# Gates of eight tokens read from PSUM key by key; the second norm closed by VectorE in halves for every token block

## The chip, the cores and the metric

The kernel runs on one core of a Trainium2 chip. Its time is the time of one execution on the device in microseconds; lower is better. One execution before the change was profiled, and three more were timed without a profile.

## The reference, cut to what matters

One decoder layer over 512 tokens of width 1024: a token mixer (attention beside a linear recurrence), a layer norm, a PEER mixture of 16384 one-neuron experts, and a second layer norm. The parts that the change touches are the gates of the experts and the last norm:

```python
sc, ci = lax.top_k(cand, PEER_TOPK)
e1 = jnp.take_along_axis(i1, ci // PEER_TOPK, axis=-1)
e2 = jnp.take_along_axis(i2, ci % PEER_TOPK, axis=-1)
experts = (e1 * PEER_N_KEYS + e2).reshape(T, PEER_HEADS * PEER_TOPK)
gates = jax.nn.softmax(sc.astype(jnp.float32), axis=-1)...
act = jax.nn.gelu(jnp.einsum('cd,ced->ce', hc, u))
return jnp.einsum('ce,ced->cd', gc * act, peer_v[ec])
...
h = layer_norm(ALPHA * h + peer_ffn(h, ...), ln2_g, ln2_b)
```

Every token has 8 heads of 16 experts with a gate each. An expert's number is a pair of keys (e1, e2) of 128 each.

## The kernel before, in words

The 512 tokens are four blocks of 128. Three blocks (384 tokens) are computed densely: the gelu of all 16384 experts is made by TensorE, 128 experts at a time (a block of the table u; there are 128 of them), multiplied by a dense matrix of gates that is zero for experts not chosen, and multiplied by the table v, 128 experts at a time. The fourth block is done by gathering its chosen rows of u and v.

**The gate stage** lies in the trace between 355 and 600 us. It goes over the 384 tokens in 48 steps of 8 tokens. `onehots` (L897 to L919) makes for each token two one-hot matrices of its chosen keys, one of them scaled by the gates (VectorE L910, L917, L918, ScalarE L916). `gate_mm` multiplies them on TensorE (L927, L928), two matmuls for each token, into the PSUM tile `psg` of 8 tokens by 128 keys, with the keys of a token side by side; there are two such tiles, in turn. Then three instructions empty the tile:

- L936, ScalarE: keys 60 to 127 (68 of them) are copied to `gst`, a staging tile in SBUF with 16 tokens side by side for each key, which a DMA (L945) writes to memory every second step, for later.
- L939, VectorE: of keys 0 to 59, those `na` whose activations were made already are multiplied into these activations, in place, in the SBUF tile `act` (60 keys by 384 tokens, tokens side by side).
- L941, ScalarE: the rest of keys 0 to 59 are copied into `act`; when their activations come, they are multiplied by them (L275, L276).

All three go through a token's keys, and then to the next token. So they read PSUM in runs along the keys, and in SBUF each element is 16 tokens (`gst`) or 384 tokens (`act`) from the one before. `na` grows from 11 in the first step to 58 in the last: L939 has 88 to 464 elements in a partition, L941 392 to 16, and L936 always 544.

Between these, TensorE makes the activations of the next u blocks (`u_mm`, L206 to L208, `psu` and `psv`), each from a block that ScalarE and VectorE split into two halves of its precision (L202, L203).

**The v stage** (to about 1361 us): for each of 128 blocks of experts ScalarE and VectorE split the block of v (L1093, L1094) and the weights (L1099, L1101), and TensorE adds the products to six accumulators (L1056, L1058). The last seven blocks are held back, and multiplied block of tokens by block of tokens, so that the accumulators of the first tokens are complete earlier.

**The end**: `finish(t)` runs for t = 0 (the gathered tokens, `gacc`), 1, 2 and 3. It adds the residual (L1143 or L1148), makes mean and variance in `layer_stats` and the reciprocal root in `rsqrt` (small VectorE instructions, L215 to L234), and then, for t below 3, a small instruction for the shift (L1158), ScalarE's scale and shift of 1024 columns (L1159), VectorE's multiplication by the gain and addition of the bias (L1160, L1161; the two rows of parameters lie in `gr`) and one DMA (L1162). For t = 3 alone it is VectorE in two halves of 512 columns: subtract the mean and multiply by the gain (L1153), multiply by the root and add the bias (L1154), and one DMA for each half from the SP and the ScalarE queues (L1155).

Each engine runs its instructions in a fixed order, which a scheduler chose when the program was built.

Of the kernel before, what the change touches and what calls it, by code (L numbers as in the profile page):

```python
# [9 lines left out]
F32 = mybir.dt.float32  # L10
# [4 lines left out]
AF = mybir.ActivationFunctionType  # L15
OP = mybir.AluOpType
AX = mybir.AxisListType.X

P = 128
S = 512  # L20
D = 1024
NT = 4
# [22 lines left out]
NW = 60  # L45
# [99 lines left out]
def _program(ctx, tc, nc, a, out, dbg, stop):  # L145
    V, A, G, T = nc.vector, nc.scalar, nc.gpsimd, nc.tensor
# [19 lines left out]
    def mk(pool, shape, dt, tag, bufs):  # L166
        uid[0] += 1
        return pool.tile(shape, dt, name=f"{tag}_{uid[0]}", tag=tag, bufs=bufs)
# [58 lines left out]
    def layer_stats(pool, src, tag):  # L227
        st = mk(pool, [P, 2, 6], F32, tag + "st", 2)
        for i in range(2):
            V.bn_stats(st[:, i], src[:, i * 512:(i + 1) * 512])  # L230
        mv = mk(pool, [P, 2], F32, tag + "mv", 2)
        V.bn_aggr(mv, st)
        ve = mk(pool, [P, 1], F32, tag + "ve", 2)
        V.tensor_scalar(ve, mv[:, 1:2], EPS, None, op0=OP.add)  # L234
        return mv, rsqrt(pool, ve, tag)
# [3 lines left out]
    def raw4():  # L239
        return mk(rp, [P, 1024], F32, "raw", RAW_BUFS)  # L240
# [383 lines left out]
    for c in range(4):  # L624
        rnn_ssq(c, sqr[c])
    V.tensor_reduce(ssq.rearrange("p t k -> p (t k)"), ssp[:, :8 * NT].rearrange("p (a g) -> p a g", g=4), axis=AX,
                    op=OP.add)
# [11 lines left out]
    for c in range(DC):  # L639
        r = raw4()  # L640
# [69 lines left out]
    pp = ctx.enter_context(tc.tile_pool(name="pp", bufs=1))  # L710
# [165 lines left out]
    NB = 8  # L876
# [44 lines left out]
    GST = {}  # L921

    def gate_mm(col0, ob, oh, ol):
        o2 = mk(PB["g"][0], [P, NB, P], F32, "psg", PB["g"][1])
        for t in range(NB):
            q = (slice(None), t // R, slice(None), t % R)
            T.matmul(o2[:, t], ob[q], oh[q], start=True, stop=False)  # L927
            T.matmul(o2[:, t], ob[q], ol[q], start=False, stop=True)  # L928
        ch, q = divmod(col0, TCH)
        if q == 0:  # L930
            GST[0] = mk(gp, [P, NKEY - NW, TCH], F32, "gst", 2)

        def part(ap):
            return ap.rearrange("p e r -> p r e")

        A.activation(part(GST[0][:, :, q:q + NB]), o2[:, :, NW:], AF.Copy)  # L936
        na = min(nact[0], NW)
        wc = W[0][:, :, col0:col0 + NB]
        V.tensor_tensor(part(wc[:, :na]), part(wc[:, :na]), o2[:, :, :na], op=OP.mult)  # L939
        if na < NW:  # L940
            A.activation(part(wc[:, na:]), o2[:, :, na:NW], AF.Copy)  # L941
        ncol[0] = col0 + NB
        if q == TCH - NB:
            i = max(i for i in range(NQ) if cut[i] <= ch)
            nc.sync.dma_start(gscr[i][:, :, ch - cut[i]].rearrange("g p e t -> p g e t"),  # L945
                              GST[0].rearrange("p (g e) t -> p g e t", e=GE))
# [52 lines left out]
    for s in range(NS):  # L999
        i, k = divmod(s, SPT)  # L1000
        if k == 0:
            gen = first[order[1]] if i == 0 else experts(order[2]) if i == 1 else iter(())
        with tc.issue_after(last[0].ins):
            steps(gen, 99 if k == SPT - 4 else 2 if k < 4 else 1)
        if k == SPT - 1 and i + 1 < ND:
            gate_prep(order[i + 1])
        nxt = onehots(order[(s + 1) // SPT], (s + 1) % SPT * NB) if s + 1 < NS else None
        if nu[0] < NW - RES:
            u_block()
        gate_mm(s * NB, *pend)  # L1010
        pend = nxt
# [11 lines left out]
    def rows(*offs, scale=None):  # L1023
        rr = []
        for off in offs:
            r = mk(dg[0], [P, D], F32, "gr", GR_BUFS)
            nc.sync.dma_start(r, rowb(off, D))
            if scale is not None:
                A.activation(r, r, AF.Copy, scale=scale)
            rr.append(r)  # L1030
        return rr
# [37 lines left out]
    for b in range(NKEY):  # L1069
# [3 lines left out]
        g, k = divmod(b - NW, GE)  # L1073
# [21 lines left out]
        if b >= NW:  # L1095
            wc = w.rearrange("p (c t) -> p c t", t=TCH)
# [6 lines left out]
        if b == NKEY - NY:  # L1103
            l2g, l2b = rows(R_L2G, R_L2B)
            l1 = rows(R_L1G, R_L1B, scale=ALPHA)
            res = {}
            for t in range(NG, NT):
                y = raw4()
# [31 lines left out]
    def finish(t):  # L1140
        if t < NG:
            y = gacc[t]
            V.tensor_tensor(y, ah[t], gacc[t], op=OP.add)  # L1143
        else:
            y = res[t]
            for hf in range(2):
                sl = slice(hf * 512, hf * 512 + 512)
                V.scalar_tensor_tensor(y[:, sl], acc[t - NG][hf], 1.0 / GS, y[:, sl], op0=OP.mult, op1=OP.add)  # L1148
        mv, ri = layer_stats(pp, y, "ln2")
        if t == NT - 1:  # L1150
            for hf in range(2):
                sl = slice(hf * 512, hf * 512 + 512)
                V.scalar_tensor_tensor(y[:, sl], y[:, sl], mv[:, 0:1], l2g[:, sl], op0=OP.subtract, op1=OP.mult)  # L1153
                V.scalar_tensor_tensor(y[:, sl], y[:, sl], ri, l2b[:, sl], op0=OP.mult, op1=OP.add)  # L1154
                (nc.sync, nc.scalar)[hf].dma_start(out[t * P:(t + 1) * P, sl], y[:, sl])  # L1155
            return
        nm = mk(pp, [P, 1], F32, "ln2nm", 2)
        V.scalar_tensor_tensor(nm, mv[:, 0:1], -1.0, ri, op0=OP.mult, op1=OP.mult)  # L1158
        A.activation(y, y, AF.Identity, scale=ri, bias=nm)  # L1159
        V.tensor_tensor(y, y, l2g, op=OP.mult)  # L1160
        V.tensor_tensor(y, y, l2b, op=OP.add)  # L1161
        nc.sync.dma_start(out[t * P:(t + 1) * P], y)  # L1162

    for t in range(NT - 1):
        finish(t)
    with tc.high_priority():
        finish(NT - 1)
# [15 lines left out]
```

## Time and profile before

| | |
|---|---|
| median of 3 runs | 1375.07 us (1374.76 to 1376.82) |
| the profiled execution | 1375.56 us |
| its span, first to last instruction | 1373.8 us |
| busy over the span: TensorE matmuls | 1327.5 us, 97% |
| VectorE | 1192.3 us, 87% |
| ScalarE | 678.6 us, 49% |
| the chain that ended last | PE 76%, DVE 18%, ACT 2%, issue 2%, DMA 2% |
| mean granted TensorE clock | 0.989 |

The span is 1.76 us shorter than the profiled execution, which is 0.49 us above the median. In the profile PE is TensorE, DVE VectorE, ACT ScalarE, and a row such as `act<-act,psg 128x384` is an instruction that reads the tiles act and psg and writes act, with 384 elements in each of 128 partitions. Matmuls overlap, so their mean durations are longer than the time from one to the next.

### The profile page before, as it was taken

How to read it: one execution, taken by the hardware profiler on the slowest of the kernel's cores; microseconds unless marked ns; L12 is line 12 of the kernel's file. 1: busy time of each engine (PE TensorE's matmuls, PEld its weight loads, DVE VectorE, ACT ScalarE, POOL GpSimd, SP SyncE). 2: the span in 40 equal slices, each digit the busy share in tenths (PEclk: the TensorE clock that was granted, in tenths of full speed). 3: DMA queues.
4: the chain of work that ended last, by engine and by line, in shares of the span. 5: the costliest groups of instructions: out<-in, count | busy, mean ns of one | idle time of the engine just before them, and what ended most of it. 6: DMA issues, size and time to landing. Idle time of an engine off the chain costs nothing.

```text
span 1373.8 us, 21409 instructions
## 1 busy us (share of the span) xinstructions
PE 1327.5 (97%) x7601; PEld 721.3 (53%) x7601; DVE 1192.3 (87%) x2555; ACT 678.6 (49%) x1155; POOL 394.8 (29%) x300
## 2 busy tenths in 40 slices
PE   8999999998999989999999999999999999999996
PEld 3554555554666656655555555555555554444442
DVE  7956766899899998989898888888898889988887
ACT  5755165434798877765433333333333333333341
POOL 0103412300000000000654545445454555545400
PEclk9998999999999999999999999999999999999998
DMA  8103053223465564665999999999999999998851
GB/s 308 64 16 123 3 176 118 93 74 123 129 167 158 145 173 135 167 228 183 394 408 396 356 355 369 364 365 366 367 361 358 351 346 365 354 330 306 305 207 74
DMA packets 142859, 332.49 MB, mean 242 GB/s; under 512 B 62880, under 2 KB 63392, under 8 KB 142752
## 3 DMA queue, kind: packets, MB, share of 16 engines
q1 hardware_dynamic: 105168, 195.59, 42.4%
q0 software_dynamic: 36864, 134.23, 26.4%
q8 instruction: 59, 0.97, 0.3%
q10 hardware_dynamic: 720, 1.31, 0.3%
q14 instruction: 48, 0.39, 0.1%
HBM read 313.53 MB, written 17.56 MB: 241 GB/s over the span
## 4 chain that ended last, share of the span: by engine, by line
PE 76%; DVE 18%; ACT 2%; issue 2%; DMA 2%; POOL 0%; DVEq 0%; SPq 0%; ACTq 0%; POOLq 0%
PE psv L1056 22%; PE psv L1058 11%; PE psu L208 8%; PE psu L206 8%; PE psu L207 8%; PE psv L206 3%; PE psv L207 3%; PE psv L208 3%; DVE wl L203 3%; DVE oab L910 2%; PE psv L475 2%; DVE k L917 1%; PE psv L661 1%; PE psv L662 1%; PE psv L663 1%
## 5 line engine op out<-in xcount | busy, mean ns | idle before, releaser
L715 POOL DMA_INDIRECT gr<-u,ei x128 | 162.7, 1271 | 524.8 <-ACT act L278 369.6
L206 PE MATMUL psu<-hh,wh 128*128 128x384 f16 (+2 forms) x816 | 265.4, 326 | 7.1 <-ACT wh L202 3.0
L208 PE MATMUL psu<-hh,wl 128*128 128x384 f16 (+1 forms) x816 | 265.7, 326 | 5.1 <-DVE wl L203 5.1
L207 PE MATMUL psu<-hl,wh 128*128 128x384 f16 (+1 forms) x816 | 265.6, 326 | 0.0
L202 ACT ACTIVATE wh<-raw 128x1024 f16<-128x1024 f32 (+1 forms) x141 | 147.8, 1048 | 193.7 <-PE psu L207 150.1
L1056 PEld LDWEIGHTS <-w_h 128*128 128x128 f16 x1536 | 150.3, 98 | 173.5
L203 DVE SCALAR_TENSOR_TENSOR wl<-raw,wh 128x1024 f16<-128x1024 f32 (+1 forms) x141 | 171.3, 1215 | 66.1 <-ACT wh L202 65.8
L715 POOL DMA_INDIRECT gr<-v,ei x128 | 170.6, 1333 | 164.7 <-DVE gacc L967 144.4
L1099 ACT ACTIVATE w_h<-act 128x384 f16<-128x384 f32 x128 | 66.1, 521 | 255.7 <-PE psv L1056 254.3
L206 PEld LDWEIGHTS <-wh 128*128 128x128 f16 x1232 | 121.4, 99 | 102.6 <-ACT wh L202 9.4
L1056 PE MATMUL psv<-vl,w_h 128*128 128x512 f16 x582 | 173.4, 379 | 0.0
L1058 PE MATMUL psv<-vh,w_l 128*128 128x512 f16 x582 | 173.4, 379 | 0.0
L208 PEld LDWEIGHTS <-wl 128*128 128x128 f16 x1232 | 121.2, 98 | 99.0 <-DVE wl L203 9.1
L1056 PE MATMUL psv<-vh,w_h 128*128 128x512 f16 x582 | 171.6, 379 | 0.0
L207 PEld LDWEIGHTS <-wh 128*128 128x128 f16 x1232 | 121.4, 99 | 94.3 <-issue 7.9
L967 DVE SCALAR_TENSOR_TENSOR gacc<-gr,gact,gacc 128x1024 f32<-128x1024 f32 x127 | 162.4, 1279 | 0.7
L957 DVE SCALAR_TENSOR_TENSOR gr<-gr,ah 128x1024 f32<-128x1024 f32 x128 | 154.0, 1216 | 1.4 <-DMA gr<-u,ei 1.3
L1094 DVE TENSOR_TENSOR vl<-rv,vh 128x1024 f16<-128x1024 f32 x97 | 118.1, 1218 | 7.6 <-ACT vh L1093 7.6
L1058 PEld LDWEIGHTS <-w_l 128*128 128x128 f16 x768 | 75.1, 98 | 90.6
L208 PE MATMUL psv<-hh,wl 128*128 128x384 f16 (+2 forms) x352 | 119.8, 342 | 1.9 <-DVE wl L203 1.9
L206 PE MATMUL psv<-hh,wh 128*128 128x384 f16 (+2 forms) x352 | 119.8, 342 | 1.5 <-ACT act L278 0.8
L207 PE MATMUL psv<-hl,wh 128*128 128x384 f16 (+2 forms) x352 | 119.9, 342 | 0.0
(264 smaller groups left out, 2050.3 us busy)
## 6 DMA issues: line engine op xcount, KB each, us to landing
raw<-uT SPq DMA_DIRECT2D x128, 512.0 KB, 4.8
rv<-v SPq DMA_DIRECT2D x98, 512.0 KB, 6.8
raw<-v SPq DMA_DIRECT2D x30, 512.0 KB, 7.1
gs<-gst SPq DMA_DIRECT2D x24, 544.0 KB, 4.2
gsb<-gs SPq DMA_DIRECT2D x34, 384.0 KB, 8.5
raw<-w_q SPq DMA_DIRECT2D x16, 512.0 KB, 4.2
raw<-w_in SPq DMA_DIRECT2D x13, 512.0 KB, 4.8
raw<-w_out SPq DMA_DIRECT2D x8, 512.0 KB, 4.3
```

The costliest lines, as they stand in the source:

```text
L202: A.activation(hi, raw, AF.Copy, scale=WS)
L203: V.scalar_tensor_tensor(lo, raw, WS, hi, op0=OP.mult, op1=OP.subtract)
L206: T.matmul(o, lh, rh, start=first, stop=False)
L207: T.matmul(o, lh, rl, start=False, stop=False)
L208: T.matmul(o, ll, rh, start=False, stop=last)
L715: G.indirect_dma_start(out=r, out_offset=None, in_=table, in_offset=bass.IndirectOffsetOnAxis(ap=idx, axis=0))
L957: V.scalar_tensor_tensor(r, r, 1.0 / ALPHA, ah[t], op0=OP.mult, op1=OP.mult, accum_out=gact[t][:, j:j + 1])
L967: V.scalar_tensor_tensor(gacc[t], r, gact[t][:, j:j + 1], gacc[t], op0=OP.mult, op1=OP.add)
L1056: T.matmul(acc[t][hf], w_h[:, tt], vv[:, hf * 512:hf * 512 + 512], start=f and vv is vh, stop=False)
L1058: T.matmul(acc[t][hf], w_l[:, tt], vh[:, hf * 512:hf * 512 + 512], start=False, stop=l)
L1094: vs = V.tensor_tensor(vl, rv, vh, op=OP.subtract)
L1099: A.activation(w_h, w, AF.Copy)
```

## The change

The three instructions that empty the gate tile go through the keys, and for each key through its eight tokens; the shapes turn from 8 x keys to keys x 8. The number of instructions, their engines and the elements that they move stay. In SBUF an instruction now meets eight neighbouring tokens (32 bytes), then the next key; in PSUM each element is 128 elements (512 bytes) from the one before. And `finish` closes every block of tokens as it closed the last one alone.

```diff
-        def part(ap):
-            return ap.rearrange("p e r -> p r e")
-
-        A.activation(part(GST[0][:, :, q:q + NB]), o2[:, :, NW:], AF.Copy)
+
+        ok = o2.rearrange("p t k -> p k t")
+        A.activation(GST[0][:, :, q:q + NB], ok[:, NW:], AF.Copy)
         na = min(nact[0], NW)
         wc = W[0][:, :, col0:col0 + NB]
-        V.tensor_tensor(part(wc[:, :na]), part(wc[:, :na]), o2[:, :, :na], op=OP.mult)
+        V.tensor_tensor(wc[:, :na], wc[:, :na], ok[:, :na], op=OP.mult)
         if na < NW:
-            A.activation(part(wc[:, na:]), o2[:, :, na:NW], AF.Copy)
+            A.activation(wc[:, na:], ok[:, na:NW], AF.Copy)
...
         mv, ri = layer_stats(pp, y, "ln2")
-        if t == NT - 1:
-            for hf in range(2):
-                sl = slice(hf * 512, hf * 512 + 512)
-                V.scalar_tensor_tensor(y[:, sl], y[:, sl], mv[:, 0:1], l2g[:, sl], op0=OP.subtract, op1=OP.mult)
-                V.scalar_tensor_tensor(y[:, sl], y[:, sl], ri, l2b[:, sl], op0=OP.mult, op1=OP.add)
-                (nc.sync, nc.scalar)[hf].dma_start(out[t * P:(t + 1) * P, sl], y[:, sl])
-            return
-        nm = mk(pp, [P, 1], F32, "ln2nm", 2)
-        V.scalar_tensor_tensor(nm, mv[:, 0:1], -1.0, ri, op0=OP.mult, op1=OP.mult)
-        A.activation(y, y, AF.Identity, scale=ri, bias=nm)
-        V.tensor_tensor(y, y, l2g, op=OP.mult)
-        V.tensor_tensor(y, y, l2b, op=OP.add)
-        nc.sync.dma_start(out[t * P:(t + 1) * P], y)
+        for hf in range(2):
+            sl = slice(hf * 512, hf * 512 + 512)
+            V.scalar_tensor_tensor(y[:, sl], y[:, sl], mv[:, 0:1], l2g[:, sl], op0=OP.subtract, op1=OP.mult)
+            V.scalar_tensor_tensor(y[:, sl], y[:, sl], ri, l2b[:, sl], op0=OP.mult, op1=OP.add)
+            (nc.sync, nc.scalar)[hf].dma_start(out[t * P:(t + 1) * P, sl], y[:, sl])
```

Lines behind the first edit move up by one (L936 becomes L935, L939 L938, L941 L940, L1094 L1093, L1148 L1147; L1153 and L1154 become L1151 and L1152).

In the gate stage no instruction changes its place on any engine; TensorE's order is the same in the whole program. A piece of VectorE's order there (`psg` is the gate tile, `oab`, `k` and `gl`, `gh` belong to the one-hot matrices, `act` are the activations):

```order
 L276 TENSOR_TENSOR act_1888<-act_1888,utmp_3664 128x16
 L910 TENSOR_TENSOR oab_3766<-iota_1895,eT_3376 128x2048
-L939 TENSOR_TENSOR act_1888<-act_1888,psg_3668 128x8x13
+L938 TENSOR_TENSOR act_1888<-act_1888,psg_3668 128x13x8
 L918 TENSOR_TENSOR k_633_3703<-oab_3700,gl_579_3384 128x512
 L917 TENSOR_TENSOR k_632_3702<-oab_3700,gh_3380 128x1024
```

Only the shape is another: 13 keys of 8 tokens instead of 8 tokens of 13 keys.

At the end VectorE's order does change. Before, from the variance of the gathered tokens (`ln2ve_13755`) to the residual of the next block (`raw_13569`; `gr_13605` and `gr_13615` are the low halves of the last two blocks of v, `gr_13559` and `gr_13561` gain and bias):

```order
L234 TENSOR_SCALAR ln2ve_13755<-ln2mv_13753 128x1
L1094 TENSOR_TENSOR gr_13605<-rv_13603,gr_13605 128x1024
...
L1094 TENSOR_TENSOR gr_13615<-raw_13613,gr_13615 128x1024
...
L1158 SCALAR_TENSOR_TENSOR ln2nm_13769<-ln2mv_13753,ln2y_13757 128x1
L1160 TENSOR_TENSOR gacc_1210_7467<-gacc_1210_7467,gr_13559 128x1024
L1161 TENSOR_TENSOR gacc_1210_7467<-gacc_1210_7467,gr_13561 128x1024
L1148 SCALAR_TENSOR_TENSOR raw_13569<-psv_6913,raw_13569 128x512
```

The same stretch now:

```order
L234 TENSOR_SCALAR ln2ve_13755<-ln2mv_13753 128x1
L1151 SCALAR_TENSOR_TENSOR gacc_1210_7467<-gacc_1210_7467,ln2mv_13753,gr_13559 128x512 x2
L1093 TENSOR_TENSOR gr_13605<-rv_13603,gr_13605 128x1024
...
L1093 TENSOR_TENSOR gr_13615<-raw_13613,gr_13615 128x1024
L216 TENSOR_SCALAR ln2y_13757<-ln2w_13758 128x1
...
L1152 SCALAR_TENSOR_TENSOR gacc_1210_7467<-gacc_1210_7467,ln2y_13757,gr_13561 128x512 x2
L1147 SCALAR_TENSOR_TENSOR raw_13569<-psv_6913,raw_13569 128x512
```

The two halves of L1151 stand ahead of the low half of v's block 126, and of the small instructions of the root only two (L215, L217) now stand ahead of that of block 127 instead of five. ScalarE's last three instructions before (L1159 for t = 0, 1 and 2) are gone, and four DMAs of half a block stand there in place of one.

## Rows read from the trace of the kernel before

**Rows 1.** Stretches: us; busy (instructions) of PE, PEld, DVE, ACT, POOL; PEclk, DMA, GB/s.

```profile
355.00:435.00 80.00, 79.17 (x674) 54.16 (x673) 76.14 (x206) 74.71 (x160) 0.00 (x0) 1.00 0.58 155
435.00:495.00 60.00, 56.70 (x449) 37.30 (x448) 59.97 (x155) 50.91 (x108) 0.00 (x0) 1.00 0.61 163
495.00:540.00 45.00, 40.51 (x321) 26.36 (x320) 40.55 (x72) 31.67 (x71) 0.00 (x0) 0.96 0.53 144
540.00:600.00 60.00, 56.94 (x462) 37.76 (x460) 53.34 (x71) 43.90 (x104) 0.00 (x0) 0.97 0.61 162
600.00:1310.00 710.00, 710.00 (x3692) 361.05 (x3690) 631.07 (x890) 281.22 (x384) 333.31 (x256) 1.00 0.94 349
```

**Rows 2.** PE groups, 355 to 600 us: busy us, mean ns | idle before, releasers.

```profile
L206 PE MATMUL psu<-hh,wh 128*128 128x384 f16 x204 | 67.6, 332 | 1.6 <-ACT act L278 1.6
...
L206 PE MATMUL psv<-hh,wh 128*128 128x384 f16 x171 | 55.7, 326 | 1.5 <-ACT act L278 0.8 <-DVE gT L886 0.7
L927 PE MATMUL psg<-k,oab 128*128 128x128 f16 x384 | 47.6, 218 | 8.0 <-DVE k L917 4.4 <-ACT gst L936 2.1 <-ACT act L941 1.1
```

**Rows 3.** Groups of L939 and L936 in the same stretch.

```profile
L939 DVE TENSOR_TENSOR act<-act,psg 128x88 f32<-128x88 f32 (+47 forms) x48 | 35.1, 735 | 2.2 <-ACT gst L936 2.2
...
L936 ACT ACTIVATE gst<-psg 128x544 f32<-128x544 f32 x48 | 50.5, 1127 | 1.6 <-PE psg L928 1.5
```

**Rows 4.** Single forms of DVE and ACT, for rates (L1097 from 600 us on).

```profile
L939 DVE TENSOR_TENSOR act<-act,psg 128x384 f32<-128x384 f32 x1 | 1.0, 987 | 0.0
...
L276 DVE TENSOR_TENSOR act<-act,utmp 128x384 f32<-128x384 f32 x1 | 0.6, 550 | 0.0
...
L276 DVE TENSOR_TENSOR act<-act,utmp 128x88 f32<-128x88 f32 x1 | 0.2, 249 | 0.0
...
L1097 DVE TENSOR_TENSOR act<-act,gsb 128x384 f32<-128x384 f32 x68 | 37.4, 550 | 0.0
...
L941 ACT ACTIVATE act<-psg 128x384 f32<-128x384 f32 x1 | 0.8, 841 | 0.0
...
L275 ACT ACTIVATE utmp<-psu 128x384 f32<-128x384 f32 x2 | 0.9, 472 | 0.0
```

**Rows 5.** L939 by stretch: 435 to 495, 495 to 540, 540 to 600 us.

```profile
L939 DVE TENSOR_TENSOR act<-act,psg 128x216 f32<-128x216 f32 (+11 forms) x12 | 8.3, 695 | 0.0
...
L939 DVE TENSOR_TENSOR act<-act,psg 128x312 f32<-128x312 f32 (+7 forms) x8 | 7.0, 881 | 0.0
...
L939 DVE TENSOR_TENSOR act<-act,psg 128x368 f32<-128x368 f32 (+12 forms) x13 | 13.8, 1072 | 1.0 <-ACT gst L936 1.0
```

**Rows 6.** Timeline of the end: start us, us, engine, instruction [idle before, releaser].

```profile
1342.76 1.22 DVE L1094 TENSOR_TENSOR gr<-raw,gr 128x1024 f16<-128x1024 f32 x1 [0.89 <-ACT gr L1093]
1342.81 1.03 PE L1056 MATMUL psv<-gr,w_h 128*128 128x512 f16 x4
...
1346.25 1.23 DVE L1160 TENSOR_TENSOR gacc<-gacc,gr 128x1024 f32<-128x1024 f32 x1 [1.31 <-ACT gacc L1159]
...
1348.66 1.28 DVE L1148 SCALAR_TENSOR_TENSOR raw<-psv,raw 128x512 f32<-128x512 f32 x2
...
1351.16 0.21 DVE L232 BATCH_NORM_AGGREGATE ln2mv<-ln2st 128x2 f32<-128x12 f32 x1
...
1360.51 0.38 PE L1058 MATMUL psv<-gr,w_l 128*128 128x512 f16 x1
...
1362.81 1.23 DVE L1160 TENSOR_TENSOR raw<-raw,gr 128x1024 f32<-128x1024 f32 x1 [0.70 <-ACT raw L1159]
...
1365.68 0.20 DVE L232 BATCH_NORM_AGGREGATE ln2mv<-ln2st 128x2 f32<-128x12 f32 x1
...
1365.99 1.40 DVE L1153 SCALAR_TENSOR_TENSOR raw<-raw,ln2mv,gr 128x512 f32<-128x512 f32 x2
1367.31 0.14 DVE L215 TENSOR_SCALAR ln2w<-ln2ve 128x1 int32<-128x1 int32 x1
...
1369.02 1.41 DVE L1154 SCALAR_TENSOR_TENSOR raw<-raw,ln2y,gr 128x512 f32<-128x512 f32 x2
```

## The prediction

> **What bounds the kernel now.** First the stretches of the span [rows 1]. From 600 to 1310 us TensorE is busy 710.00 of 710 us, so a microsecond won before 600 us moves all of this forward, and nothing that ScalarE or VectorE save inside it counts; the change touches nothing there. In the gate stage, 355 to 600 us, TensorE stands 0.8, 3.3, 4.5 and 3.1 us in the four stretches (length less busy time), 11.7 us in all, and the granted clock falls to 0.96 and 0.97 in the last two: 45 x 0.04 + 60 x 0.03 = 3.6 us of full-speed time. VectorE is busy 76.14 of 80 and 59.97 of 60 us in the first two, 40.55 of 45 and 53.34 of 60 us in the others; ScalarE has 201.2 of 245. So VectorE paces the middle of the stage and TensorE the rest of it, nearly level. Next, what TensorE waited for there [rows 2]: 8.0 us ahead of the gate matmuls (4.4 for VectorE's one-hot product L917, 2.1 for L936 and 1.1 for L941, which hold the gate tile) and the other 3.7 us ahead of u's matmuls, mostly for ScalarE's L278. L939 and L936 are thus part of what it waits for: 35.1 us of VectorE and 50.5 us of ScalarE [rows 3]. Last the end [rows 6]: TensorE's last matmul starts at 1360.51 us, but VectorE still normalises the blocks before, and reaches the last block's variance (L232) only at 1365.68. The end hangs on VectorE.
>
> **The gate tile: what an element costs.** With 384 elements L939 takes 987 ns, and the same multiplication of neighbouring elements, L276, 550 [rows 4]. L276 goes from 249 ns at 88 elements to 550 at 384, 1.02 ns an element over about 160 ns, so an element of L939 costs (987 - 160)/384 = 2.15 ns. ScalarE shows the same: L941 841 ns, L275 472, with equal elements. In both slow rows PSUM is read side by side and SBUF is touched far apart, so SBUF is what doubles the price. Short runs in SBUF are not dear: L1097 reads gsb in runs of 16 tokens at 550 ns, as fast as L276 [rows 4]. Runs of eight floats should do as well.
>
> What no row shows is a read of PSUM with 512 bytes between elements. Its cost lies between about 1.0 ns, the price of a PSUM read side by side (L1148 of the end, 1.28 us for two times 512 [rows 6], with 0.1 us taken off for each), and 2.15 ns, what SBUF takes for far elements; nothing excludes more. I take 1.02. The reason is an estimate: from 600 to 1310 us 3692 matmuls of 384 or 512 columns fill 710 us [rows 1], 0.192 us each, so PSUM takes at least 384/192 = 2.0 columns in a nanosecond. An engine that draws one element in 1.02 ns asks for half of that, and could do so even if a far element spoiled its neighbour's place.
>
> [...]
>
> **What it saves.** L939 at 160 + 1.02 ns an element, by stretch [rows 5]: 12 instructions of 260 elements on average go from 695 to 425 ns, 3.2 us; 8 of 340 from 881 to 507, 3.0 us; 13 of 416 from 1072 to 584, 6.3 us. TensorE stood 3.3, 4.5 and 3.1 us there, so the smaller of the two in each is 3.2 + 3.0 + 3.1 = 9.3 us. I take four fifths, 7.5 us: in the last two stretches VectorE itself stood idle 4.5 and 6.7 us, so some waits are chains between engines that a faster L939 shortens only in part. The first stretch, with 0.8 us of idle TensorE, I leave out, and the clock too. ScalarE's saving is larger, about 0.5 us for each of 48 L936 (1127 x 472/841 = 630 ns), 24 us, but ScalarE has 44 us to spare; it counts through the gate tile, which comes free sooner. Bounds of this term: nothing, and 11.7 + 3.6 = 15 us. The staging DMA starts earlier and moves the same bytes; no order changes in this stage.
>
> **The end, followed row by row** [rows 6]. From one start to the next, a pair of halves costs 1.32 us (L1153 at 1365.99, L215 at 1367.31) and the root from L215 to the pair behind it 1.71 (to 1369.02). L1151 for the gathered tokens now stands ahead of the low halves of v's last two blocks. Its 1.32 us, less three small instructions that move behind, fit into the 0.89 us for which VectorE waited for ScalarE before the second low half, so that one starts at 1342.76 as before, and the first is done by then. TensorE comes to these two blocks at 1342.81 and uses the low half third, at about 1343.2: it isn't delayed. From 1342.76: 1.14 for the low half (its 1.22 less the 0.08 by which neighbours overlap, as in the 1.40 of L1153's pair), 1.54 for what is left of the root (without L215 and L217), 1.32 for L1152. So the next block's residual (L1148, now L1147) begins at 1346.76 instead of 1348.66; the 1.31 us wait for ScalarE ahead of L1160 is gone. A block then costs 2.50 for residual and statistics (1348.66 to L232 at 1351.16), 0.31 from L232 to L1151 (as 1365.68 to 1365.99), 1.32, 1.71 and 1.32 again: 7.16 us, and the block after it begins at 1353.92. That one takes the same and, among its small instructions, the first half of the last block's residual and statistics, 1.25 more: 1362.33. TensorE's last matmul starts at 1360.51 and takes 0.38, so it isn't waited for. The last half of residual and statistics, 1.25, and L232 starts at 1363.58 instead of 1365.68. What follows is the same. **2.1 us** off. Bounds: nothing, if six smaller DMAs on two queues in place of three delay the last two, and 3.5 us, where TensorE's end (1360.89 + 1.25) would bind. ScalarE's queue then holds DMAs alone, so their waits delay nobody.
>
> **Sum.** 1375.56 (the profiled execution) - 7.5 - 2.1 = 1365.96 us. This execution lay 0.49 us above the median of the runs, so I forecast **1365.5 us**.
>
> **Rivals.**
> - PSUM read far apart costs what SBUF did, 2.15 ns. For it: nothing in the trace shows the contrary, and two memories beside one engine may be built alike. Against it: the matmul estimate. The gate stage stays, the end gives 2.1: 1375.07 - 2.1 = 1373.0 us.
> - The reads are cheap, but TensorE's waits stay for the most part, since u's chain (L275 waits for L276, L278 lets u's matmuls go) and ScalarE are late next. For it: 3.7 of 11.7 us of waits are not ahead of gate matmuls [rows 2]. Against it: L276 stands behind L939 on VectorE. A third of the 7.5, and the 2.1: 1370.5 us.
> - Slower: a far PSUM element costs more than a far SBUF element, say another 1.02 ns. L939 meets 12 x 260 + 8 x 340 + 13 x 416 = 11248 elements where VectorE paces, which is 11.5 us more, and less the 2.1 of the end 1375.07 + 9.4 = 1384.5 us. It decides from 2.1 us / 11248 = 0.19 ns above the present 2.15 on. For it: each key's eight tokens lie 512 bytes apart over the whole tile, a pattern no row has. Against it: the slow SBUF rows stop at twice the price.
>
> **Chances and range.** Cheap reads and the waits go: 0.45. Cheap reads, waits mostly stay: 0.12. Price as now: 0.30. Dearer: 0.13. What a measurement can tell from no change is about 0.2%, 2.75 us. The first two are faster (0.57), the third, 2.1 us, is within it (0.30), the last is slower (0.13). The range goes from 1361.5 (11.5 us in the gate stage and the 2.1) to 1375.5, which holds the third case with a lost end; left out are the dearer case and a gain near the bound of 15. The forecast's own range is 1361.5 to 1369.
>
> **What would show it.** Right: L936's successor near 0.63 us and L939's at 384 elements near 0.55; TensorE idle under 5 us between 355 and 600 us, and the v stage about 7 us earlier; L232 of the last block about 2.1 us nearer to TensorE's end than its 5.2 us (1360.51 to 1365.68), with no wait for ScalarE among the blocks. Wrong: these durations at 1.1 and 0.99 us or above, or shorter ones with TensorE idle as before.

## The result, and the profile after

| | before | after |
|---|---|---|
| median | 1375.94 us (4 runs, 1374.76 to 1377.52) | 1361.2 us (4 runs, 1359.69 to 1361.63) |
| the profiled execution | 1375.56 us | 1361.63 us |
| its span | 1373.8 us | 1359.9 us |
| TensorE / VectorE / ScalarE busy | 1327.5 / 1192.3 / 678.6 us | 1323.4 / 1179.7 / 653.4 us |

The ratio to before is 0.9885, with a 95% interval of 0.9873 to 0.9897: 14.2 to 17.5 us faster. I had forecast 1365.5 us, 9.6 less, in a range that began at 1361.5. The direction and the mechanism held; what TensorE wins in the gate stage was sized too small.

TensorE runs the same 7601 matmuls in the same order in both kernels, so the start of one and the same matmul in the two traces tells where the time went:

| matmul that starts before at | after at | difference | won since the row above |
|---|---|---|---|
| 355.12 us | 356.74 us | +1.61 | |
| 435.16 | 435.97 | +0.81 | 0.8 |
| 495.08 | 491.77 | -3.30 | 4.1 |
| 540.05 | 533.37 | -6.68 | 3.4 |
| 600.03 | 588.49 | -11.54 | 4.9 |
| 1310.00 | 1298.46 | -11.54 | 0.0 |
| last, 1360.51 | 1348.97 | -11.54 | 0.0 |
| end of the span, 1373.8 | 1359.9 | -13.9 | 2.4 |

The gate stage gave 13.2 us, the end 2.4; the 1.6 us lost ahead of 355 us are a difference between two executions: in the other runs below this number goes from 0.4 to 3.5 us, where nothing was changed either. In this execution of the changed kernel the granted clock was 0.83 from 190 to 200 us and from 340 to 350 us, where it was 1.00 before. From 600 us on the difference stays the same until TensorE is done.

The price of the elements, in the lines of the changed kernel that answer to [rows 3, 4] (the groups of the gate stage, and single forms):

```profile
L938 DVE TENSOR_TENSOR act<-act,psg 128x88 f32<-128x88 f32 (+47 forms) x48 | 20.6, 431 | 0.1
...
L935 ACT ACTIVATE gst<-psg 128x544 f32<-128x544 f32 x48 | 29.5, 628 | 6.4 <-PE psg L928 6.0
L940 ACT ACTIVATE act<-psg 128x392 f32<-128x392 f32 (+47 forms) x48 | 15.2, 324 | 1.8 <-DVE act L938 1.8
...
L938 DVE TENSOR_TENSOR act<-act,psg 128x384 f32<-128x384 f32 x1 | 0.5, 547 | 0.0
...
L940 ACT ACTIVATE act<-psg 128x384 f32<-128x384 f32 x1 | 0.5, 471 | 0.0
```

VectorE's 384 elements take 547 ns instead of 987, about as many as L276 takes for neighbours in SBUF (550); ScalarE's take 471 instead of 841, as L275 does (472); and L935 takes 628 instead of 1127. The 512 bytes between elements in PSUM add nothing that these rows show: ScalarE's L275 reads PSUM side by side, and takes 472 ns where L940 takes 471. VectorE gives up 35.1 - 20.6 = 14.5 us, ScalarE's L936 50.5 - 29.5 = 21 us.

What TensorE waited for from 355 to 600 us (the PE groups with idle time before them), and the four stretches of [rows 1]:

```profile
L206 PE MATMUL psu<-hh,wh 128*128 128x384 f16 x224 | 73.0, 326 | 0.5 <-ACT act L278 0.5
L208 PE MATMUL psu<-hh,wl 128*128 128x384 f16 x223 | 72.7, 326 | 0.8 <-DVE wl L203 0.8
...
L206 PE MATMUL psv<-hh,wh 128*128 128x384 f16 x175 | 57.0, 326 | 0.9 <-DVE gT L886 0.7 <-ACT act L278 0.2
L927 PE MATMUL psg<-k,oab 128*128 128x128 f16 x384 | 47.0, 218 | 1.0 <-DVE k L917 1.0
```

```profile
355.00:435.00 80.00, 79.83 (x679) 54.63 (x678) 76.44 (x210) 67.12 (x161) 0.00 (x0) 1.00 0.58 162
435.00:495.00 60.00, 60.00 (x495) 40.52 (x494) 59.93 (x161) 46.85 (x114) 0.00 (x0) 1.00 0.62 169
495.00:540.00 45.00, 42.40 (x342) 28.00 (x341) 39.91 (x73) 31.16 (x81) 0.00 (x0) 1.00 0.56 156
540.00:600.00 60.00, 59.62 (x469) 39.19 (x468) 51.90 (x88) 43.21 (x105) 0.00 (x0) 1.00 0.68 205
```

Ahead of the gate matmuls 1.0 us is left of 8.0 [rows 2], and neither gate-tile copy of ScalarE is named any more. The granted clock is 1.00 in the last two stretches, where it was 0.96 and 0.97. In the second stretch VectorE is as busy as before (59.93 us, 59.97 then), but TensorE no longer waits for it: it is busy 60.00 of 60 us.

The end, from the changed kernel's timeline:

```profile
1333.71 1.42 DVE L1152 SCALAR_TENSOR_TENSOR gacc<-gacc,ln2y,gr 128x512 f32<-128x512 f32 x2
1335.04 1.28 DVE L1147 SCALAR_TENSOR_TENSOR raw<-psv,raw 128x512 f32<-128x512 f32 x2
...
1348.97 0.38 PE L1057 MATMUL psv<-gr,w_l 128*128 128x512 f16 x1
...
1350.49 0.68 DVE L1147 SCALAR_TENSOR_TENSOR raw<-psv,raw 128x512 f32<-128x512 f32 x1
1351.20 0.69 DVE L230 BATCH_NORM_STATS2 ln2st<-raw 128x6 f32<-128x512 f32 x1
1351.93 0.21 DVE L232 BATCH_NORM_AGGREGATE ln2mv<-ln2st 128x2 f32<-128x12 f32 x1
```

The last block's variance comes 2.96 us behind TensorE's last matmul, where it came 5.17 behind [rows 6]; I had counted 3.07.

### The profile page after: what moved, and what is told of

It reads as the page before. It is cut to its first block, busy times and chain, and to the rows that moved or that the text cites. A ratio compares the mean times of both kernels' runs of the same rounds, so it can differ in the third digit from the quotient of the medians.

```text
span 1359.9 us, 21413 instructions
## 1 busy us (share of the span) xinstructions
PE 1323.4 (97%) x7601; PEld 721.2 (53%) x7601; DVE 1179.7 (87%) x2558; ACT 653.4 (48%) x1152; POOL 396.0 (29%) x300
## 4 chain that ended last, share of the span: by engine, by line
PE 81%; DVE 13%; ACT 2%; issue 2%; DMA 1%; POOL 1%; DVEq 0%; SPq 0%; ACTq 0%
PE psv L1055 22%; PE psv L1057 11%; PE psu L206 8%; PE psu L207 8%; PE psu L208 8%; PE psv L206 4%; PE psv L208 4%; PE psv L207 4%; DVE wl L203 3%; DVE oab L910 2%; PE psv L475 1%; PE psv L773 1%; DVE k L917 1%; PE psv L661 1%; PE psv L662 1%
## 5 line engine op out<-in xcount | busy, mean ns | idle before, releaser
L1093 DVE TENSOR_TENSOR vl<-rv,vh 128x1024 f16<-128x1024 f32 x97 | 118.2, 1219 | 7.4 <-ACT vh L1092 7.4
```

The source lines that it names most:

```text
L1093: vs = V.tensor_tensor(vl, rv, vh, op=OP.subtract)
```

## The experiments

Ratios are to the kernel before, timed beside each of them, with their 95% intervals. Two theories stood against each other for the gate stage: that VectorE's busy time paces it, so that L939 carries the gain; and that the gate tile was held too long, and ScalarE's L936, first of those that free it, carries it.

**The two edits apart.** The first kernel has the first hunk of the diff alone, the second the second hunk alone.

> The three instructions of the gate stage changed, the end as before. If the two edits stand beside each other without touching: 12 to 13 us faster (the same work of TensorE from 355 to 600 us took 13.2 us less in the changed kernel), about 1363 us, with the last block's L232 5.2 us behind TensorE's last matmul as before. If part of the gain behind 600 us needs the shorter end, less than 10 us.

Measured: 1365.4 us, 0.9914 (0.9899 to 0.9928), 9.9 to 13.9 us faster. The same stretches as in the table above gave 0.81, 4.11, 3.37 and 4.86 us, equal to the changed kernel within 0.01 us, and the span ends 13.4 us behind TensorE's last matmul, as before (13.3).

> The end changed alone. By the row-by-row count 2.1 us faster, with TensorE's last matmul at about 1360 us and L232 of the last block about 3.1 us behind it. Rival, that the six smaller DMAs eat it: within 0.5 us of before.

Measured: 1374.56 us, 0.998 (0.9971 to 0.999), 1.4 to 4.0 us faster. The last matmul starts at 1361.53 and L232 at 1364.77:

```profile
1361.53 0.38 PE L1058 MATMUL psv<-gr,w_l 128*128 128x512 f16 x1
```

```profile
1364.77 0.21 DVE L232 BATCH_NORM_AGGREGATE ln2mv<-ln2st 128x2 f32<-128x12 f32 x1
```

3.24 us instead of 5.17, 1.9 less, and the span ends 11.2 us behind the last matmul instead of 13.3: the smaller DMAs take nothing back. Each edit alone gives in its place about what it gives in the changed kernel.

**Each instruction of the gate tile alone.** In each of these kernels one of the three reads key by key and the others stay as before:

```diff
-        A.activation(part(GST[0][:, :, q:q + NB]), o2[:, :, NW:], AF.Copy)
+        A.activation(GST[0][:, :, q:q + NB], o2.rearrange("p t k -> p k t")[:, NW:], AF.Copy)
```

> Only L936 (ScalarE, keys 60 to 127, always 544 elements) reads key by key. If VectorE's busy time paces the stage: ScalarE gives up 24 us and TensorE's waits hardly shrink, 1 to 3 us faster. Rival, that the gate tile is held too long and L936 stands first in what frees it: 6 us or more.

Measured: 1374.05 us, 0.9979 (0.9967 to 0.9992), 1.1 to 4.5 us faster. L936 fell to 632 ns, and TensorE's wait for it is gone, but not that for VectorE (PE group, 355 to 600 us):

```profile
L927 PE MATMUL psg<-k,oab 128*128 128x128 f16 x384 | 47.3, 218 | 5.7 <-DVE k L917 5.4 <-ACT act L941 0.3
```

It was 4.4 for L917 before [rows 2] and is 5.4 now: where ScalarE is no longer late, VectorE is.

```diff
-        V.tensor_tensor(part(wc[:, :na]), part(wc[:, :na]), o2[:, :, :na], op=OP.mult)
+        V.tensor_tensor(wc[:, :na], wc[:, :na], o2.rearrange("p t k -> p k t")[:, :na], op=OP.mult)
```

> Only L939 (VectorE) reads key by key. If VectorE's busy time paces the stage: 14.5 us less of it, 8 to 10 us faster. Rival, that the gate tile is held too long by ScalarE: 3 us or less, with TensorE still waiting for L936 and L941.

Measured: 1366.53 us, 0.9928 (0.9915 to 0.9941), 8.1 to 11.7 us faster: most of the whole gate edit's 11.8 (9.9 to 13.9). The gate matmuls' group, with L936 at 1135 ns as before:

```profile
L927 PE MATMUL psg<-k,oab 128*128 128x128 f16 x384 | 47.1, 218 | 2.0 <-DVE k L917 1.2 <-ACT act L941 0.8
```

```profile
L936 ACT ACTIVATE gst<-psg 128x544 f32<-128x544 f32 x48 | 50.7, 1135 | 2.8 <-PE psg L928 2.7
```

L936 stayed dear, and still TensorE doesn't wait for it: the 2.1 us of [rows 2] went with L939 alone. That ScalarE's hold of the gate tile carries the gain falls as the main cause. L939 holds the tile as well, but no wait of TensorE between 355 and 600 us was put down to L939 in the kernel before; what fell most is the wait for L917, which VectorE runs behind it, from 4.4 to 1.2 us.

> Only L941 (ScalarE, 392 down to 16 elements) reads key by key. If VectorE's busy time paces the stage: 9 us less of ScalarE, which has 44 us to spare, and at most 1 us faster. Rival, that the hold of the gate tile matters whoever holds it: 2 us or more, as with L936 alone.

The edit is the same on L941. Measured: 1375.12 us, 0.9987 (0.9979 to 0.9996), 0.6 to 2.9 us faster. The interval takes in both answers. The three gains alone add up to 2.9 + 9.9 + 1.8 = 14.6 us against 11.8 together, by the middle of their intervals, which are too wide to tell the two apart. By the starts of the same matmuls in the traces the stretch from 355 to 600 us is 3.7, 10.8 and 2.3 us shorter, 16.8 in all, against 13.15 together: they overlap rather than help each other.

**How short the runs may be.** The changed kernel with the eight tokens in passes of four or two over the keys; the two other instructions likewise:

```diff
-        ok = o2.rearrange("p t k -> p k t")
-        A.activation(GST[0][:, :, q:q + NB], ok[:, NW:], AF.Copy)
+        ok = o2.rearrange("p (a b) k -> p a k b", b=4)
+
+        def runs(ap):
+            return ap.rearrange("p k (a b) -> p a k b", b=4)
+
+        A.activation(runs(GST[0][:, :, q:q + NB]), ok[:, :, NW:], AF.Copy)
...
-        V.tensor_tensor(wc[:, :na], wc[:, :na], ok[:, :na], op=OP.mult)
+        V.tensor_tensor(runs(wc[:, :na]), runs(wc[:, :na]), ok[:, :, :na], op=OP.mult)
```

> The changed kernel with the eight tokens in two passes over the keys of four each: runs of 16 bytes in SBUF instead of 32. If a far SBUF element costs only when its neighbours in the same 16 bytes are not used: L938 with 384 elements stays at 0.55 us and L935 at 0.63, and the time at 1361 us. If each jump costs an element's time: 0.65 us or more (one jump in four elements), 1363 us or more.

Measured: 1361.32 us, 0.989 (0.9875 to 0.9905). The multiplication is L942 here:

```profile
L942 DVE TENSOR_TENSOR act<-act,psg 128x384 f32<-128x384 f32 x1 | 0.5, 546 | 0.0
```

> The same with four passes of two tokens each: runs of 8 bytes. The scheduler moves instructions here, so the durations decide and not the time. [...] If each jump costs an element's time: about 0.75 us; if runs must fill 16 bytes: near 0.99, as before.

Measured: 1364.38 us, 0.9916 (0.9899 to 0.9932), with other orders on TensorE, VectorE and ScalarE. The durations:

```profile
L942 DVE TENSOR_TENSOR act<-act,psg 128x384 f32<-128x384 f32 x1 | 0.5, 548 | 0.0
```

```profile
L939 ACT ACTIVATE gst<-psg 128x544 f32<-128x544 f32 x48 | 30.6, 638 | 4.8 <-PE psg L928 4.7
```

With runs of two floats the multiplication of 384 elements takes 548 ns, neither 0.75 us nor 0.99; with runs of eight it takes 547. ScalarE's 544 elements take 638 ns, with runs of eight 628. So four times as many jumps in SBUF came with 1 ns more on VectorE and 10 on ScalarE; what costs is a float alone in its place, with which the same instructions took 987 and 1127 ns.

**What is left in the stage.** The changed kernel with `na = 3 * NB // 4` in `onehots` instead of `NB // 2`:

> The changed kernel with the low one-hot halves of six of eight tokens on ScalarE (L916) instead of four: VectorE's L918 shrinks from 512 to 256 elements, about 0.14 us less in each of 48 steps, 6.7 us; ScalarE gets 96 more L916 of about 0.33 us, 32 us, of the 57 it has to spare in the changed kernel. If VectorE still paces what is left of TensorE's waits (4 us): 1 to 3 us faster than 1361. If ScalarE takes its place: as fast or up to 5 us slower, with TensorE waiting for L916 and L278.

Measured: 1368.37 us, 0.9939 (0.992 to 0.9957), slower than the changed kernel. TensorE now waits for ScalarE (its two largest waits):

```profile
L206 PE MATMUL psu<-hh,wh 128*128 128x384 f16 x207 | 68.3, 330 | 3.8 <-ACT act L278 3.6
...
L927 PE MATMUL psg<-k,oab 128*128 128x128 f16 x384 | 46.8, 218 | 1.5 <-ACT act L940 1.5
```

ScalarE had time to spare over the stage (in the changed kernel it is busy 188.3 of 245 us), but TensorE waits for it at the places where the work was put; 2.2 us were lost against the kernel before between 355 and 435 us alone, and the span ends 11.2 us behind the last matmul, about as in the changed kernel (10.9). The scheduler also set the gate and u matmuls of TensorE in another order from 396 us on, so how much of the loss is ScalarE's and how much the order's is not shown.

**The end further.** The changed kernel with GpSimd closing the norm of the first blocks (for t below 2, and for t = 0 alone):

```diff
         mv, ri = layer_stats(pp, y, "ln2")
+        if t < 2:
+            nm = mk(pp, [P, 1], F32, "ln2nm", 2)
+            V.scalar_tensor_tensor(nm, mv[:, 0:1], -1.0, ri, op0=OP.mult, op1=OP.mult)
+            A.activation(y, y, AF.Identity, scale=ri, bias=nm)
+            G.tensor_tensor(y, y, l2g, op=OP.mult)
+            G.tensor_tensor(y, y, l2b, op=OP.add)
+            nc.sync.dma_start(out[t * P:(t + 1) * P], y)
+            return
```

> The changed kernel, with the norm of t = 0 and 1 closed by ScalarE (scale and shift) and then GpSimd (gain and bias), and t = 2 and 3 by VectorE in halves. VectorE gives up about 4 us of work behind 1328 us. TensorE's end then binds: its last matmul starts at 1348.97 and takes 0.38, and the last half of residual and statistics 1.25, so L232 comes at about 1350.6 instead of 1351.93: 1.3 us faster than the changed kernel. Rival, that GpSimd beside VectorE slows VectorE's instructions (L1147 over 0.64 us for 512): as fast or slower.

Measured: 1363.59 us, 0.99 (0.9884 to 0.9917).

> The same for t = 0 alone: VectorE gives up two pairs of halves, of which the first stood partly in a wait, so about 1.3 us. L232 of the last block at about 1350.6: 1.3 us faster than the changed kernel, with less of GpSimd beside VectorE. Rival as there.

Measured: 1364.29 us, 0.9906 (0.9889 to 0.9922).

> The changed kernel again on this chip, to set the two beside: 0.9885 of before, within 0.002.

Measured: 1360.29 us, 0.9887 (0.9868 to 0.9906). Both GpSimd versions lie above it, but the intervals overlap, and 2.0 and 3.1 us of the distance between the profiles lie ahead of 355 us, where nothing was changed. The ends decide: 12.3 and 11.9 us from TensorE's last matmul to the end of the span, against 10.7. So the rival came true, and the 1.3 us were not won. In the version for two blocks, the timelines of GpSimd and of VectorE show why:

```profile
1342.78 2.35 POOL L1153 TENSOR_TENSOR raw<-raw,gr 128x1024 f32<-128x1024 f32 x1 [2.21 <-ACT raw L1152]
1345.21 2.68 POOL L1154 TENSOR_TENSOR raw<-raw,gr 128x1024 f32<-128x1024 f32 x1
```

```profile
1344.17 4.27 DVE L1159 SCALAR_TENSOR_TENSOR raw<-raw,ln2mv,gr 128x512 f32<-128x512 f32 x2
```

VectorE's pair of halves, 1.40 us elsewhere, takes 4.27 beside GpSimd's two instructions. The rows read as a wait rather than as a slower pace: its second half starts while GpSimd's second instruction runs, and ends 0.55 us behind that one's end at 1347.89.

```profile
1345.61 2.83 DVE L1159 SCALAR_TENSOR_TENSOR raw<-raw,ln2mv,gr 128x512 f32<-128x512 f32 x1
```

Even an instruction of one column, 0.22 us elsewhere, that starts within GpSimd's takes 2.19 and ends with it (same version, for t = 0):

```profile
1338.23 2.34 POOL L1154 TENSOR_TENSOR gacc<-gacc,gr 128x1024 f32<-128x1024 f32 x1
1338.40 2.19 DVE L220 SCALAR_TENSOR_TENSOR ln2w<-ln2y,ln2h 128x1 f32<-128x1 f32 x1
```

In the version for t = 0 alone the pair that meets GpSimd's second instruction takes 3.49 and ends 0.5 us behind it:

```profile
1338.67 2.86 POOL L1154 TENSOR_TENSOR gacc<-gacc,gr 128x1024 f32<-128x1024 f32 x1
```

```profile
1338.58 3.49 DVE L1159 SCALAR_TENSOR_TENSOR raw<-raw,ln2mv,gr 128x512 f32<-128x512 f32 x2
```

The statistics beside GpSimd's first instruction were not stretched (version for two blocks):

```profile
1342.54 1.28 DVE L230 BATCH_NORM_STATS2 ln2st<-raw 128x6 f32<-128x512 f32 x2
```

No kernel that was run is faster than the changed one; runs of four are equal to it.

## Why the prediction was right or wrong

**The price of an element** was right on the two sides: 1.02 ns and about 160 ns fixed gave 0.55 us for 384 elements (547 ns), and the ratio of ScalarE's two rows 0.63 for L936 (628). The choice between 1.02 and 2.15 ns was the one that decided. The price was measured, its reason was not: no run tests whether what matmuls write into PSUM in a nanosecond says anything of what VectorE and ScalarE can read. At 547 ns, where a price as before would have left 987, the rivals of a price as before and of a dearer one fall.

**VectorE's saving** was right: 3.2, 3.0 and 6.3 us were forecast for the last three stretches, and the same instructions gave 3.4, 3.0 and 6.0 (the forecast counted the one of 368 elements in two stretches); over all it was 14.5 us. That VectorE's time is what TensorE's waits hang on was right too: L939 alone gave 9.9 of 11.8 us.

**What TensorE wins from it** was the step that failed: 7.5 us were put down, 13.2 came. It was the rule "the smaller of saving and wait in each stretch, and four fifths of that", with the first stretch and the clock left out. Between the same matmuls of the two traces, with a wait where the time from one start to the next exceeds that of the columns at a clock of 1.00 (512 start 0.216 us apart between 600 and 1310 us, 0.42 ns a column) by over 0.25 us, and the rest being smaller excesses:

| stretch | forecast before the four fifths | won | of it waits | of it the rest |
|---|---|---|---|---|
| 355 to 435 us | left out | 0.8 | 0.8 | 0.0 |
| 435 to 495 | 3.2 | 4.1 | 3.9 | 0.2 |
| 495 to 540 | 3.0 | 3.4 | 2.3 | 1.1 |
| 540 to 600 | 3.1 | 4.9 | 3.2 | 1.7 |
| sum | 9.3 | 13.2 | 10.2 | 3.0 |

The miss of 5.7 us has three parts. The four fifths took 1.8 us off, on the ground that VectorE stood idle in the last two stretches and some waits were chains; but the waits that went there are 9.4 us, by the sum the 9.3 that stood before the four fifths, though not stretch by stretch. The first stretch, left out, gave 0.8. And the rest column, 3.0, is what I had written down as 3.6 us of full-speed time and not counted: it stands in the last two stretches, where the clock was 0.96 and 0.97 and is 1.00 now. In all 10.2 of 14.4 us of waits went.

In the kernel before, the clock fell right behind waits of TensorE: to 0.71 in 505 to 510 us, with 3.48 of 5 us busy, and to 0.90 and 0.76 in 585 to 595, where the wait of 2.15 us for L936 had ended at 587.83.

```profile
505.00:510.00 5.00, 3.48 (x24) 1.87 (x24) 5.00 (x11) 3.84 (x7) 0.00 (x0) 0.71 0.44 130
...
585.00:590.00 5.00, 2.85 (x33) 2.12 (x31) 5.00 (x8) 4.26 (x9) 0.00 (x0) 0.90 0.48 139
590.00:595.00 5.00, 5.00 (x25) 2.68 (x24) 2.26 (x3) 1.46 (x6) 0.00 (x0) 0.76 0.89 215
```

Whether the clock came back because the waits went, the profiles leave open. In the eight with L939 changed and four tokens on ScalarE it is 1.00 in both stretches. But it can be 1.00 with the waits in place, too. From 540 to 600 us it is 0.97 before and with the end alone, and 1.00 in the eleven others, and one of these is the kernel with L941 alone, where TensorE is busy 56.94 us as before and has the same wait of 2.15 us:

```profile
540.00:600.00 60.00, 56.94 (x472) 38.23 (x471) 55.03 (x74) 44.73 (x107) 0.00 (x0) 1.00 0.63 166
```

```profile
589.23 0.22 PE L927 MATMUL psg<-k,oab 128*128 128x128 f16 x1 [2.15 <-ACT gst L936]
```

That stretch was 1.7 us shorter there, with no wait less. From 495 to 540 us it is 0.96 before, with L936 alone, with L941 alone and with six tokens on ScalarE; it is 1.00 with the end alone, with the waits in place, and that stretch was 0.5 us shorter there. So 2.2 of the 3.0 us were won in kernels whose waits had stayed, and may be a difference between executions. Shown as won by the change are the 10.2 us of waits.

**The rival that TensorE's waits mostly stay** was wrong: of the 8.0 us ahead of the gate's matmuls 1.0 is left, and of the 3.7 ahead of u's 2.2.

**The end** was right: 2.1 us forecast; 1.9 to 2.2 in the distance of L232 from the last matmul, 2.4 in the span of the changed kernel. L1147 of the next block did start 1.14 + 1.54 + 1.32 = 4.0 us behind the start of the low half of v's last block (1331.05 to 1335.04), and VectorE did not wait for TensorE: the last matmul had ended, at 1348.97 + 0.38, before VectorE came to the last half of the residual at 1350.49.

**The sum.** 13.15 and 2.39 us, less 1.61 us of difference between the executions ahead of the gate stage, are the 13.9 us between the two profiles. The measured 1361.2 us lies 0.3 us under the forecast's range, whose lower end I had set at 11.5 us for the gate stage, though its bound, worked out from the same rows, was 15. The 0.3 us are less than the 0.5 and 1.7 us that came with a clock of 1.00 in kernels whose waits had stayed; that the term of the gate stage was too small does not hang on it.

## What to carry to other kernels

Lay the order of an instruction so that SBUF is met in neighbours, two floats at least, and let PSUM take the jumps: here that nearly halved the durations of three instructions (987 to 547 ns, 841 to 471, 1127 to 628). Where two engines are nearly level, a shorter instruction on the one that paces gives TensorE the waits that it causes elsewhere too; here the smaller of saving and wait, stretch by stretch, was the right sum without a discount (9.3 us against 9.4). Time at the lower clock behind such waits may come back as well (3.0 us here, of which 2.2 came in kernels whose waits had stayed): give it a place in the range, up to its whole amount. Work that is moved to an engine with time to spare can land where TensorE then waits for it (3.6 us for ScalarE's L278 in the stage), or hold up the engine that it was to relieve (4.27 us instead of 1.40 for VectorE's pair beside GpSimd).

## What the runs showed of the hardware that was not expected

VectorE's pair of halves went from 1.40 us to 4.27 and 3.49 beside GpSimd's products and sums of 1024 floats (2.34 to 2.86 us each). I had listed slower instructions as a rival, but not a wait for the end of GpSimd's whole instruction, as the rows read: 2.83 us for a half, and 2.19 instead of 0.22 us for one column. Each of these instructions of VectorE reads two SBUF tiles; the statistics, which read one, kept their 1.28 us beside GpSimd. That the number of tiles sets them apart is not shown: in the kernel before, a cast of one tile with 768 columns (L733), started at 201.02 us within GpSimd's 2.25 us of L200 (from 200.84), took 2.49, where a cast of 256 columns just ahead of it took 0.29. The size of the wait is about what is left of GpSimd's instruction: the half lost 2.1 us with 2.3 left, the one column 2.0 with 2.2.

And runs of two floats in SBUF are as cheap as runs of eight (548 and 547 ns for 384 elements), with PSUM 512 bytes apart within a run.
